# Experts' weights as 1 MB blocks of two neighbouring rows per partition, weight storage in 8 KB tiles

## The chip, the cores and the metric

The kernel runs on one core of one Trainium2 chip. The metric is the device time of one execution in microseconds (us). The engines are named as in the profile: PE multiplies matrices, PEld is its weight load, DVE, ACT and POOL are the vector, scalar and GpSimd engines, and SP issues the DMAs.

## What is computed

Two transformer blocks run one after the other on 512 tokens of width 1024, all in float32. The first block has two layers. Each layer has a mixer (latent attention beside a convolution), an attention over 256 memory rows, and a gated feed-forward part of width 2816. The second block is one layer: a gated delta-rule mixer with a pooling branch, and then a mixture of 16 experts. Each expert takes the 64 tokens with its highest affinity:

```python
aff = jax.nn.softmax((h @ w_router).astype(jnp.float32), axis=-1)
top_aff, top_idx = lax.top_k(jnp.swapaxes(aff, 1, 2), cap)          # cap = 2*512//16 = 64
xe = jax.vmap(lambda hb, ib: hb[ib])(h, top_idx)
hid = jax.nn.silu(einsum('becd,edf->becf', xe, w_gate)) * einsum('becd,edf->becf', xe, w_up)
ye = einsum('becf,efd->becd', hid, w_down) * top_aff[..., None]
# ... each expert's rows are added back to their tokens, scaled by a gate vector; then a final RMS norm
```

Each expert has three weight matrices of 1024 x 1024 in float32, so 48 matrices of 4 MB are read once.

## The kernel before, in words

The program is written as plain loops over tiles. A planner beneath it puts the instructions of each engine and of SP in an order, by its own costs and by when a tile's buffer is free; so an order in the trace need not be that of the source. A tile is asked for by a tag, and a tag has a fixed number of buffers. A buffer is free again when every instruction that touches its tile is done.

**Weights outside the experts.** `weight` (line 134) loads a piece of up to 128 x 1024 elements into a tile `wr` (5 buffers of 4 KB per partition), copies it rounded to a tile `wh` on ACT (line 148), and puts the rest into a tile `wl` on DVE or POOL (line 152). `wh` and `wl` have 4 buffers of 4 KB each. Three matmuls (`mm3`, lines 157 to 159) make one product. `kv_weight` (line 535) does the same for one matrix. `adaln` (line 902) loads its 48 pieces of `w_mod` into `wr` and multiplies them on DVE.

**The delta-rule part.** `delta_block` is run for eight blocks, four at a time (`lockstep`, line 1236). Each of the four has a scratch store for the whole of its run and passes it to the block that comes four later. The store is a `wr` buffer, taken by `block_store` (line 1229), and four are taken. Beside the blocks run the four `pool_branch` calls, one after the other. Each takes three tiles `s2` (11 buffers for all users), loads a small weight of 64 KB through `weight`, and multiplies. `delta_scan` follows.

**The experts** (`moe`, line 1614). `gather(q)` builds the inputs of four experts: the normalised tokens (two parts, `hh` and `hl`) are PE's stationary operand, and a 0/1 selection is the moving one (line 1732). ACT applies a scale and a shift per feature (line 1734). Feature k*128+p of the model lies on partition p of slice k. `hidden(e)` multiplies one expert's inputs by `w_gate` and `w_up`. The moving operand is a weight block in float32; the stationary one is 128 x 64, and each block is used by two matmuls that write the two halves of the partitions of one PSUM bank (lines 1762 and 1763):

```python
for ps, w in ((pg, A["w_gate_2"]), (pu, A["w_up_2"])):
    halves(ps, xe[:, k, e % 4, :], block(w, e, k), k == 0, k == 7)
```

Then come SiLU, a product, four transposes and a copy. `project(p)` multiplies two experts' results by `w_down` (line 1791). `combine(p)` adds the pair's rows to the tokens (line 1804 on PE, line 1812 on DVE), and `prepare(p)` makes the pair's combine matrix. In the loop `hidden(e)` comes first, then for even e `prepare` and the `project` of the pair before, for odd e its `combine`.

`block(w, e, k)` (line 1661) issues one DMA of 512 KB, 128 rows of 4 KB, one per partition. It goes to the next of 24 buffers of 4 KB per partition, taken in turn (`room`): 5 `wr`, 4 `wh`, 4 `wl`, one `nx`, and 10 halves of five larger tiles. There are 16 blocks for an expert's `hidden` and 8 for its part of `project`, 384 in all.

Of the kernel before, what the change touches and what calls it, by code (L numbers as in the profile page):

```python
# [10 lines left out]
F32 = mybir.dt.float32  # L11
F32R = mybir.dt.float32r
# [5 lines left out]
D = 1024  # L18
# [37 lines left out]

class Builder:
    N_N4 = 4
    N_WR = 5
    N_WH = 4  # L60

    def __init__(self, ctx, tc, A, out, dbg):
        self.tc, self.nc, self.A, self.out, self.dbg = tc, tc.nc, A, out, dbg
        self.cp = ctx.enter_context(tc.tile_pool(name="consts", bufs=1))
        self.sp = ctx.enter_context(tc.tile_pool(name="main", bufs=1))
        self.pp = ctx.enter_context(tc.tile_pool(name="psum", bufs=1, space=bass.MemoryType.PSUM))
        self.dp = ctx.enter_context(tc.tile_pool(name="dram", bufs=1, space=bass.MemoryType.DRAM))
        self.nw = 0
# [12 lines left out]
        self.xt = self.cp.tile([128, NT, D], F32, name="xt")  # L81
# [44 lines left out]
    def split_ps(self, ps, hi, lo, scale=None):  # L126
# [4 lines left out]
        else:  # L131
            nc.vector.scalar_tensor_tensor(lo, ps, scale, hi.bitcast(F32), op0=OP.mult, op1=OP.subtract)

    def weight(self, src, shape, raw=None, spare=False):

        nc = self.nc
        loaded = raw is not None
        if not loaded:
            raw = self.sp.tile([128] + list(shape), F32, name="wr", tag="wr", bufs=self.N_WR)
        if spare:  # L140
            hi, lo = self.n4(shape, F32R), self.n4(shape, F32R)
        else:
            hi = self.sp.tile([128] + list(shape), F32R, name="wh", tag="wh", bufs=self.N_WH)
        if not loaded:
            nc.sync.dma_start(raw, src)
        i = self.nw
        self.nw += 1
        nc.scalar.activation(hi, raw, AF.Copy)  # L148
        if not spare:
            lo = self.sp.tile([128] + list(shape), F32R, name="wl", tag="wl", bufs=self.N_WH)  # L150
# [287 lines left out]
    def mixer(self, l, xT):  # L438
# [94 lines left out]
        w_ukv = A["mla_w_ukv"][l].rearrange("(k p) (h d) -> p k h d", p=128, h=8)  # L533

        def kv_weight(d0):
            raw = self.sp.tile([128, 2, 512], F32, name="wr", tag="wr", bufs=self.N_WR)
            hi = self.sp.tile([128, 2, 512], F32R, name="wh", tag="wh", bufs=self.N_WH)
            lo = self.sp.tile([128, 2, 512], F32R, name="wl", tag="wl", bufs=self.N_WH)
# [363 lines left out]
    def adaln(self):  # L902
# [10 lines left out]
        for cc in range(12):  # L913
            cs = slice(cc * 512, (cc + 1) * 512)
            rs = (0, 1) if cc < 4 else (0,)
            acc = [self.s2([512]) for _ in rs]
            for k in range(0, 8, 2):
                wt = self.sp.tile([128, 2, 512], F32, name="wr", tag="wr", bufs=self.N_WR)
# [12 lines left out]
            nc.sync.dma_start(bm[0:1, :], A["b_mod_2"][0:1, cs])  # L931
            for r in rs:
                ps = self.pc()
                nc.tensor.matmul(ps[0:1, :], self.ones, acc[r], start=True, stop=True)
                o = self.s2([512])
                nc.vector.tensor_tensor(out=o[0:1, :], in0=ps[0:1, :], in1=bm[0:1, :], op=OP.add)
                nc.sync.dma_start(self.mod[r:r + 1, cs], o[0:1, :])
            yield

    def vectors2(self):  # L940
# [13 lines left out]
            nc.sync.dma_start(rows[8 + 16 * r:24 + 16 * r, :], k(self.mod[r, 0:2 * D]))  # L954
        nc.sync.dma_start(rows[40:48, :], k(A["norm2_2"][0]))
        nc.sync.dma_start(rows[48:64, :], k(self.mod[0, 3 * D:5 * D]))
        ps = self.pc()
        self.tr(ps[:, :64], rows[:64, :])
        v = self.c2.tile([128, 64], F32, name="mv")
        nc.vector.tensor_copy(v, ps[:, :64])  # L960

        wr = self.n4([8, 16])
        nc.sync.dma_start(wr, A["w_router_2"][0].rearrange("(k p) e -> p k e", p=128))
# [4 lines left out]
        self.rc = self.c2.tile([128, 16], F32, name="rc")  # L968
        nc.vector.tensor_copy(self.rc, ps[:, :16])

        a2 = self.c2.tile([128, 8], F32, name="a2")
        self.m2 = a2, v[:, 48:56]
# [256 lines left out]
    def block_store(self, w=None):  # L1229

        if w is None:
            w = self.sp.tile([128, 2, 4, 128], F32, name="wr", tag="wr", bufs=self.N_WR)
        self.nc.gpsimd.memset(w[:, 1], 0.0)
        return w

# [378 lines left out]
    def moe(self, cat):  # L1614
# [12 lines left out]
        def done(t, c):  # L1627
# [11 lines left out]
            if c == 0:  # L1639
# [11 lines left out]
        self.dump("x2", self.xt)  # L1651


        room = [self.sp.tile([128, D], F32, name=n, tag=n, bufs=k)
                for n, k in (("wr", self.N_WR), ("wh", self.N_WH), ("wl", self.N_WH), ("nx", 1)) for _ in range(k)]
        for _ in range(5):
            raw = self.t8([2, D], F32)
            room += [raw[:, 0], raw[:, 1]]
        turn = [0]

        def block(w, e, k):

            raw = room[turn[0] % len(room)]
            turn[0] += 1
            nc.sync.dma_start(raw, w[0, e, k * 128:(k + 1) * 128, :])
            return raw

        self.stage("wout")
# [48 lines left out]
        def gather(q):  # L1717
# [8 lines left out]
            for k in range(0, 8, 2):  # L1726
                ps = gring().rearrange("p (j n) -> p j n", j=2)
                for j in range(2):
                    ks = slice((k + j) * 128, (k + j + 1) * 128)
                    for i, src in enumerate((hh, hl)):  # L1730
                        for t in range(NT):
                            mm(ps[:, j, :], src[t // 2][:, t % 2, ks], oh[t // 2][:, t % 2],  # L1732
                               start=i + t == 0, stop=i + t == NT)
                    nc.scalar.activation(xe[:, k + j].rearrange("p e c -> p (e c)"), ps[:, j, :], AF.Identity,
                                         scale=a2[:, k + j:k + j + 1], bias=sh[:, k + j:k + j + 1])
                yield

        def prepare(p):
# [25 lines left out]

        def hidden(e, tokens=None):
            pg, pu = uring(), uring()
            for k in range(8):
                if tokens is not None and k % 2 == 0:
# [7 lines left out]
            ps = mring()  # L1776
            for j in range(4):
# [5 lines left out]
        def project(p):  # L1783

            hT = [hTs.pop(2 * p + j) for j in range(2)]
            pss = [dring(), dring()]
            for k in range(8):
                raw = [block(A["w_down_2"], 2 * p + j, k) for j in range(2)]
                for ps, cs in zip(pss, (c0, c1)):
                    for j, h in enumerate((lo_, hi_)):  # L1790
                        mm(ps[h, :], hT[j][:, k % 4, k // 4, :], raw[j][:, cs], start=k == 0, stop=k == 7)  # L1791
# [136 lines left out]
```

## Time and profile before

| | |
|---|---|
| time, three runs | 2574.59 us median (2574.55 to 2577.21) |
| profiled execution: its time / its span | 2574.39 us / 2572.2 us |
| mean granted PE clock | 0.975 |
| busy share of the span | PE 94%, PEld 70%, DVE 51%, ACT 35%, POOL 24% |
| DMA | 393.79 MB, mean 153 GB/s |

The profile is of one execution. "Busy" is the time an engine has an instruction in hand. The span is cut into 40 equal slices of 64.3 us, and a digit is the busy share of a slice in tenths. The experts' stage is the last eight of these slices. A wait is named by the instruction that waits and by what released it.

### The profile page before, as it was taken

How to read it: one execution, taken by the hardware profiler on the slowest of the kernel's cores; microseconds unless marked ns; L12 is line 12 of the kernel's file. 1: busy time of each engine (PE TensorE's matmuls, PEld its weight loads, DVE VectorE, ACT ScalarE, POOL GpSimd, SP SyncE). 2: the span in 40 equal slices, each digit the busy share in tenths (PEclk: the TensorE clock that was granted, in tenths of full speed). 3: DMA queues.
4: the chain of work that ended last, by engine and by line, in shares of the span. 5: the costliest groups of instructions: out<-in, count | busy, mean ns of one | idle time of the engine just before them, and what ended most of it. 6: DMA issues, size and time to landing. Idle time of an engine off the chain costs nothing.

```text
span 2572.2 us, 32232 instructions
## 1 busy us (share of the span) xinstructions
PE 2428.2 (94%) x12518; PEld 1795.3 (70%) x12518; DVE 1305.6 (51%) x2180; ACT 898.9 (35%) x1611; POOL 612.9 (24%) x467
## 2 busy tenths in 40 slices
PE   7989999999998979998999999989889789999997
PEld 6747888777777847887888888878788644343432
DVE  3977446754547785646554343466667511112112
ACT  4673442222222584433335343263562311010101
POOL 2872112221113583103122111223415000000000
PEclk9999999999999999999999999999889889999999
DMA  5312421554543311522232222221001489999996
GB/s 164 91 42 81 149 84 57 189 156 156 172 153 106 102 49 50 155 92 82 85 107 91 82 87 78 67 75 51 20 26 50 179 310 378 409 408 409 409 409 267
DMA packets 207060, 393.79 MB, mean 153 GB/s; under 512 B 24016, under 2 KB 115288, under 8 KB 206908
## 3 DMA queue, kind: packets, MB, share of 16 engines
q1 hardware_dynamic: 206908, 391.74, 43.7%
q8 instruction: 98, 1.61, 0.3%
q14 instruction: 54, 0.44, 0.0%
HBM read 389.56 MB, written 2.13 MB: 152 GB/s over the span
## 4 chain that ended last, share of the span: by engine, by line
PE 81%; DVE 12%; ACT 3%; DMA 2%; issue 1%; POOL 1%; SPq 0%; DVEq 0%; POOLq 0%; ACTq 0%
PE q L157 17%; PE q L159 17%; PE q L158 17%; PE q L1762 8%; PE q L1791 6%; PE q L163 3%; PE q L1732 2%; PE q L1804 1%; DVE wl L152 1%; PE q L1188 1%; PE q L1183 1%; DVE q L670 1%; PE q L1763 1%; DVE xt L281 1%; DVE s L1159 1%
## 5 line engine op out<-in xcount | busy, mean ns | idle before, releaser
L157 PE MATMUL q<-t,wh 128*128 128x512 f32 (+1 forms) x1320 | 491.7, 374 | 9.7 <-DVE t L130 4.4
L158 PE MATMUL q<-t,wh 128*128 128x512 f32 (+1 forms) x1320 | 491.0, 372 | 1.9 <-DVE t L1484 1.1
L159 PE MATMUL q<-t,wl 128*128 128x512 f32 (+1 forms) x1320 | 488.8, 372 | 0.5 <-DVE wl L152 0.5
L148 ACT ACTIVATE wh<-wr 128x1024 fp32r<-128x1024 f32 (+3 forms) x280 | 288.9, 1034 | 505.4 <-PE q L159 214.5
L157 PE MATMUL q<-wh,t 128*128 128x512 f32 (+4 forms) x964 | 365.5, 383 | 14.1 <-ACT wh L148 4.8
L152 DVE TENSOR_TENSOR wl<-wr,wh 128x1024 fp32r<-128x1024 f32 (+3 forms) x206 | 263.8, 1282 | 222.7 <-ACT wh L148 217.4
L158 PE MATMUL q<-wl,t 128*128 128x512 f32 (+4 forms) x964 | 362.1, 377 | 2.6 <-POOL wl L152 1.4
L159 PE MATMUL q<-wh,t 128*128 128x512 f32 (+4 forms) x964 | 358.6, 378 | 0.4 <-POOL t L1484 0.2
L152 POOL TENSOR_TENSOR wl<-wr,wh 128x1024 fp32r<-128x1024 f32 (+2 forms) x74 | 183.9, 2486 | 636.8 <-ACT wh L148 587.7
L157 PEld LDWEIGHTS q<-t,wh 128*128 128x128 f32 x1320 | 251.1, 191 | 58.3 <-DVE t L130 4.9
L158 PEld LDWEIGHTS q<-t,wh 128*128 128x128 f32 x1320 | 251.3, 190 | 44.5 <-DVE t L1484 1.4
L159 PEld LDWEIGHTS q<-t,wl 128*128 128x128 f32 x1320 | 251.2, 190 | 42.0 <-DVE wl L152 1.4
L185 POOL TENSOR_TENSOR sm<-sm,mhalf 128x1 f32<-128x1 f32 (+3 forms) x75 | 71.8, 959 | 768.8 <-DVE sm L183 764.8
L157 PEld LDWEIGHTS q<-wh,t 128*128 128x128 f32 x964 | 183.5, 191 | 57.3 <-DVE xt L292 6.0
L158 PEld LDWEIGHTS q<-wl,t 128*128 128x128 f32 x964 | 183.7, 191 | 34.8 <-POOL wl L152 1.9
L159 PEld LDWEIGHTS q<-wh,t 128*128 128x128 f32 x964 | 182.7, 190 | 35.5 <-issue 0.9
L680 POOL TENSOR_TENSOR t<-t,cm 128x511 f32<-128x511 f32 (+14 forms) x120 | 147.9, 1233 | 22.3 <-ACT cm L677 16.8
L801 POOL TENSOR_TENSOR t<-cm,t 128x512 fp32r<-128x512 f32 x44 | 70.4, 1600 | 303.3 <-ACT t L800 303.3
L163 PE MATMUL q<-ident,s 128*128 128x128 f32 (+3 forms) x506 | 90.6, 287 | 50.4 <-DVE s L1694 13.1
L163 PEld LDWEIGHTS q<-ident,s 128*128 128x128 f32 (+3 forms) x506 | 60.6, 143 | 104.6 <-ACT s L609 26.5
L1763 PE MATMUL q<-t,t 128*64 128x512 f32 x272 | 127.6, 600 | 0.0
L1762 PE MATMUL q<-t,t 128*64 128x512 f32 x272 | 127.2, 598 | 0.0
(445 smaller groups left out, 3665.0 us busy)
## 6 DMA issues: line engine op xcount, KB each, us to landing
wr<-in_ffn_w_in SPq DMA_DIRECT2D x88, 512.0 KB
t<-in_w_gate SPq DMA_DIRECT2D x68, 512.0 KB
t<-in_w_up SPq DMA_DIRECT2D x68, 512.0 KB
wr<-in_w_mod SPq DMA_DIRECT2D x48, 512.0 KB
wr<-in_ffn_w_down SPq DMA_DIRECT2D x44, 512.0 KB
wr<-in_w_down SPq DMA_DIRECT2D x35, 512.0 KB
wr<-in_xa_w_kv SPq DMA_DIRECT2D x32, 512.0 KB
wl<-in_w_down SPq DMA_DIRECT2D x32, 512.0 KB
```

Of the source, the lines that this page charges most:

```text
L148: nc.scalar.activation(hi, raw, AF.Copy)
L152: e.tensor_tensor(out=lo, in0=raw, in1=hi.bitcast(F32), op=OP.subtract)
L157: m(out, ah, bh, start=first, stop=False)
L158: m(out, ah, bl, start=False, stop=False)
L159: m(out, al, bh, start=False, stop=last)
L163: self.nc.tensor.transpose(out, in_, self.ident[:n, :n])
L185: nc.gpsimd.tensor_tensor(out=r, in0=v, in1=self.mhalf[:, :n], op=OP.pow)
L680: nc.gpsimd.tensor_tensor(out=acc[:, i, d:], in0=acc[:, i, d:], in1=m, op=OP.add)
L801: nc.gpsimd.tensor_tensor(out=hl[:, j + i, :], in0=sg, in1=hh[:, j + i, :].bitcast(F32), op=OP.subtract)
L1762: mm(ps[lo_, :], x, raw[:, c0], start=first, stop=last)
L1763: mm(ps[hi_, :], x, raw[:, c1], start=first, stop=last)
L1791: mm(ps[h, :], hT[j][:, k % 4, k // 4, :], raw[j][:, cs], start=k == 0, stop=k == 7)
```

## The change

**Blocks.** `block(w, e, j)` loads 256 rows of a matrix as 1 MB: partition p takes the two neighbouring rows 256j+2p and 256j+2p+1, which lie one behind the other in memory. There are 192 blocks. `room` has 12 buffers of 8 KB: 3 `wr`, 4 `wh` and five larger tiles; `nx` and `wl` are gone. Each block is used for its first rows and then for its second (r = 0, 1).

**Order of the features.** So that operands fit, `gather` takes every second feature as stationary operand (a step of two elements), the transposes in `hidden` read every second column, and the scale and shift vectors are needed in that order as well: `vectors2` loads them a second time with six small DMAs, and its transposed tile has 88 columns instead of 64.

**Storage.** `wr` has 3 buffers of 8 KB, and `raw4` hands out their halves in turn, across all users. `wh` has 4 buffers of 8 KB that hold both parts, the rounded one and the rest.

```diff
-    N_WR = 5
+    N_WR = 3
+    def raw4(self, shape):
+        if self.nraw % 2 == 0:
+            self.rawt = self.sp.tile([128, 2, D], F32, name="wr", tag="wr", bufs=self.N_WR)
+        half = self.rawt[:, self.nraw % 2, :int(np.prod(shape))]
+        self.nraw += 1
+        return half if len(shape) == 1 else half.rearrange("p (a b) -> p a b", a=shape[0])
+    def parts(self, shape):
+        t = self.sp.tile([128, 2, D], F32R, name="wh", tag="wh", bufs=self.N_WH)
+        out = [t[:, i, :int(np.prod(shape))] for i in range(2)]
+        ...
     def weight(self, src, shape, raw=None, spare=False):
...
-            raw = self.sp.tile([128] + list(shape), F32, name="wr", tag="wr", bufs=self.N_WR)
+            raw = self.raw4(shape)
...
-            hi = self.sp.tile([128] + list(shape), F32R, name="wh", tag="wh", bufs=self.N_WH)
+            hi, lo = self.parts(shape)
...
     def block_store(self, w=None):
-            w = self.sp.tile([128, 2, 4, 128], F32, name="wr", tag="wr", bufs=self.N_WR)
+            w = self.raw4([1024]).rearrange("p (a b c) -> p a b c", a=2, b=4)
...
     # vectors2
+        for i, ap in enumerate((A["norm2_2"][0], self.mod[0, 3 * D:4 * D], self.mod[0, 4 * D:5 * D])):
+            for r in range(2):
+                nc.sync.dma_start(rows[64 + 8 * i + 4 * r:68 + 8 * i + 4 * r, :],
+                                  ap.rearrange("(j p r) -> r j p", p=128, r=2)[r])
...
     # moe
-        def block(w, e, k):
+        def block(w, e, j):
...
-            nc.sync.dma_start(raw, w[0, e, k * 128:(k + 1) * 128, :])
+            nc.sync.dma_start(raw, w[0, e, j * 256:(j + 1) * 256, :].rearrange("(p r) d -> p r d", r=2))
...
     # gather
+                            x = src[t // 2][:, t % 2].rearrange("p (j q r) -> p j r q", q=128, r=2)
+                            mm(ps[:, r, :], x[:, j, r, :], oh[t // 2][:, t % 2], start=i + t == 0, stop=i + t == NT)
...
     # hidden
-                    halves(ps, xe[:, k, e % 4, :], block(w, e, k), k == 0, k == 7)
+                    raw = block(w, e, j)
+                    for r in range(2):
+                        halves(ps, xe[:, 4 * r + j, e % 4, :], raw[:, r], j + r == 0, j + r == 4)
...
-                self.tr(ps[:, j * 128:(j + 1) * 128], u[:, j * 128:(j + 1) * 128])
+                self.tr(ps[:, j * 128:(j + 1) * 128], uv[:, j // 2, j % 2, :])
...
     # project
-            for k in range(8):
-                raw = [block(A["w_down_2"], 2 * p + j, k) for j in range(2)]
+            for i in range(4):
+                raw = [block(A["w_down_2"], 2 * p + j, i) for j in range(2)]
+                for r in range(2):
+                    for ps, cs in zip(pss, (c0, c1)):
+                        for j, h in enumerate((lo_, hi_)):
+                            mm(ps[h, :], hT[j][:, i % 2 * 2 + r, i // 2, :], raw[j][:, r, cs],
+                               start=i + r == 0, stop=i + r == 4)
```

The places in `kv_weight` and `adaln` that took a `wr` tile call `raw4` in the same way, and the first calls `parts`.

## Rows read from the trace of the kernel before

**Rows 1.** The page: span, busy time per engine, DMA share in 40 slices
```profile
span 2572.2 us, 32232 instructions
...
PE 2428.2 (94%) x12518; PEld 1795.3 (70%) x12518; DVE 1305.6 (51%) x2180; ACT 898.9 (35%) x1611; POOL 612.9 (24%) x467
...
DMA  5312421554543311522232222221001489999996
```

**Rows 2.** The page: chain that ended last, by engine
```profile
PE 81%; DVE 12%; ACT 3%; DMA 2%; issue 1%; POOL 1%; SPq 0%; DVEq 0%; POOLq 0%; ACTq 0%
```

**Rows 3.** Windows: from:to, length, busy PE PEld DVE ACT POOL (count), clock, DMA share, GB/s
```profile
480.00:540.00 60.00, 60.00 (x250) 45.46 (x249) 40.68 (x55) 14.30 (x17) 16.25 (x6) 1.00 0.53 167
...
1860.00:1940.00 80.00, 73.08 (x658) 68.66 (x657) 52.01 (x117) 49.42 (x126) 12.19 (x10) 0.87 0.07 21
...
2065.00:2553.00 488.00, 486.26 (x2076) 191.92 (x2076) 82.25 (x150) 51.91 (x87) 0.00 (x0) 0.99 0.98 389
...
2220.00:2260.00 40.00, 39.99 (x166) 14.61 (x165) 7.86 (x16) 3.55 (x6) 0.00 (x0) 1.00 1.03 409
```

**Rows 4.** Waits of PEld, 2200 to 2545: who for what, us, times, longest
```profile
PEld q L1762 <- issue: 61.5, 209, 0.8
...
PEld q L1762 <- DMA wr<-in_w_down: 3.7, 13, 0.3
...
PEld q L1791 <- DMA t<-in_w_down: 1.8, 3, 0.8
```

**Rows 5.** Waits of SP's own queue, 2000 to 2560
```profile
SPq L1665 <- PE q L1763: 81.9, 101, 19.2
SPq L1665 <- DMA t<-in_w_up: 45.7, 52, 0.9
```

**Rows 6.** Timeline: buffer nx loaded, read, loaded anew (start, duration, idle before)
```profile
2276.28 0.33 SPq L1665 DMA_DIRECT2D nx<-in_w_up  x1
...
2305.34 0.14 PEld L1762 LDWEIGHTS q<-nx,t 128*64 128x64 f32 x1 [0.29 <-DMA wh<-in_w_down]
2305.77 0.14 PEld L1762 LDWEIGHTS q<-nx,t 128*64 128x64 f32 x1 [0.29 <-issue]
...
2306.84 0.33 SPq L1665 DMA_DIRECT2D nx<-in_w_down  x1
```

**Rows 7.** Timeline of SP: two loads issued one after the other
```profile
2322.02 0.33 SPq L1665 DMA_DIRECT2D wr<-in_w_up  x1
2323.30 0.33 SPq L1665 DMA_DIRECT2D wr<-in_w_gate  x1
```

**Rows 8.** The chain in order of time, at the end: start, us, what
```profile
2539.33 13.88 PE q L1791 x60
```

**Rows 9.** Groups by line and form, 2100 to 2540: busy us, mean ns
```profile
L1732 PEld LDWEIGHTS q<-s,t 128*128 128x128 f32 x192 | 24.5, 189 | 20.3 <-issue 19.5 <-ACT t L1734 0.8
```

**Rows 10.** Line 1142: stationary operand is one column repeated; ns min/median/max
```profile
L1142 PEld LDWEIGHTS q<-trif,gla x48: 185/190/192, 1376.8 to 1884.5; 128*128 128x128 f32 x48
```

**Rows 11.** Two lines of vectors2: SP's issues
```profile
L956 SPq DMA_DIRECT2D s<-mod x1: 309/309/309, 1153.7 to 1153.7; - x1
...
L963 SPq DMA_DIRECT2D n<-in_w_router x1: 368/368/368, 1233.8 to 1233.8; - x1
```

**Rows 12.** The page: the split of weights on ACT, count and idle time
```profile
L148 ACT ACTIVATE wh<-wr 128x1024 fp32r<-128x1024 f32 (+3 forms) x280 | 288.9, 1034 | 505.4 <-PE q L159 214.5
```

**Rows 13.** Waits of SP's own queue, 1780 to 1990
```profile
SPq L1372 <- POOL s L1419: 26.3, 2, 21.2
```

**Rows 14.** Lines of pool_branch on DVE: ns min/median/max, first to last start
```profile
L1413 DVE TENSOR_TENSOR s<-n,s x2: 675/684/693, 1830.2 to 1907.0; 128x512 f32<-128x512 f32 x2
...
L1414 DVE TENSOR_TENSOR s<-s,t x2: 691/796/900, 1838.8 to 1907.7; 128x512 f32<-128x512 f32 x2
...
L1419 DVE TENSOR_TENSOR s<-s,s x2: 681/687/693, 1845.2 to 1935.0; 128x512 fp32r<-128x512 f32 x2
```

**Rows 15.** Timeline of PEld where combine cuts in
```profile
2215.67 0.19 PEld L1804 LDWEIGHTS q<-n,s 128*128 128x128 f32 x1 [0.81 <-ACT n L1796]
```

More of the change, by code (lines that the diff above doesn't have):

```diff
@@ L67, in __init__ @@
         self.dp = ctx.enter_context(tc.tile_pool(name="dram", bufs=1, space=bass.MemoryType.DRAM))
-        self.nw = 0
+        self.nw = self.nraw = 0
         self.wp, self.np, self.c2 = None, 0, self.cp
@@ L132, in split_ps @@
             nc.vector.scalar_tensor_tensor(lo, ps, scale, hi.bitcast(F32), op0=OP.mult, op1=OP.subtract)
+    def raw4(self, shape):
[7 more added lines that the diff above has]
+        out = [t[:, i, :int(np.prod(shape))] for i in range(2)]
+        return out if len(shape) == 1 else [x.rearrange("p (a b) -> p a b", a=shape[0]) for x in out]
     def weight(self, src, shape, raw=None, spare=False):
@@ L148, in weight @@
         nc.scalar.activation(hi, raw, AF.Copy)
-        if not spare:
-            lo = self.sp.tile([128] + list(shape), F32R, name="wl", tag="wl", bufs=self.N_WH)
         e = nc.gpsimd if self.pool_lo and i % self.pool_lo == self.pool_lo - 1 else nc.vector
@@ L535, in kv_weight @@
         def kv_weight(d0):
-            raw = self.sp.tile([128, 2, 512], F32, name="wr", tag="wr", bufs=self.N_WR)
-            hi = self.sp.tile([128, 2, 512], F32R, name="wh", tag="wh", bufs=self.N_WH)
-            lo = self.sp.tile([128, 2, 512], F32R, name="wl", tag="wl", bufs=self.N_WH)
+            raw = self.raw4([2, 512])
+            hi, lo = self.parts([2, 512])
             for k in range(2):
@@ L917, in adaln @@
             for k in range(0, 8, 2):
-                wt = self.sp.tile([128, 2, 512], F32, name="wr", tag="wr", bufs=self.N_WR)
+                wt = self.raw4([2, 512])
                 nc.sync.dma_start(wt, w[k * 128:(k + 2) * 128, cs].rearrange("(k p) f -> p k f", p=128))
@@ L956, in vectors2 @@
         nc.sync.dma_start(rows[48:64, :], k(self.mod[0, 3 * D:5 * D]))
+        for i, ap in enumerate((A["norm2_2"][0], self.mod[0, 3 * D:4 * D], self.mod[0, 4 * D:5 * D])):
+            for r in range(2):
+                nc.sync.dma_start(rows[64 + 8 * i + 4 * r:68 + 8 * i + 4 * r, :],
+                                  ap.rearrange("(j p r) -> r j p", p=128, r=2)[r])
         ps = self.pc()
-        self.tr(ps[:, :64], rows[:64, :])
-        v = self.c2.tile([128, 64], F32, name="mv")
-        nc.vector.tensor_copy(v, ps[:, :64])
+        self.tr(ps[:, :88], rows[:88, :])
+        v = self.c2.tile([128, 88], F32, name="mv")
+        nc.vector.tensor_copy(v, ps[:, :88])
         wr = self.n4([8, 16])
@@ L969, in vectors2 @@
         nc.vector.tensor_copy(self.rc, ps[:, :16])
-        a2 = self.c2.tile([128, 8], F32, name="a2")
-        self.m2 = a2, v[:, 48:56]
+        a2p = self.c2.tile([128, 8], F32, name="a2")
+        self.m2 = a2p, v[:, 72:80]
+        nc.vector.scalar_tensor_tensor(a2p, v[:, 80:88], 1.0, v[:, 64:72], op0=OP.add, op1=OP.mult)
+        a2 = self.sm([8])
         nc.vector.scalar_tensor_tensor(a2, v[:, 56:64], 1.0, v[:, 40:48], op0=OP.add, op1=OP.mult)
@@ L1651, in moe @@
         self.dump("x2", self.xt)
[L1654 to L1658, printed above, removed]
+        room = [self.sp.tile([128, 2, D], F32, name=n, tag=n, bufs=k)
+                for n, k in (("wr", self.N_WR), ("wh", self.N_WH)) for _ in range(k)]
+        room += [self.t8([2, D], F32) for _ in range(5)]
         turn = [0]
-        def block(w, e, k):
+        def block(w, e, j):
             raw = room[turn[0] % len(room)]
             turn[0] += 1
-            nc.sync.dma_start(raw, w[0, e, k * 128:(k + 1) * 128, :])
+            nc.sync.dma_start(raw, w[0, e, j * 256:(j + 1) * 256, :].rearrange("(p r) d -> p r d", r=2))
             return raw
@@ L1725, in gather @@
             a2, sh = self.m2
[L1726 to L1729, printed above, removed]
+            for j in range(4):
+                ps = gring().rearrange("p (r n) -> p r n", r=2)
+                for r in range(2):
                     for i, src in enumerate((hh, hl)):
                         for t in range(NT):
[L1732 to L1735, printed above, removed]
+                            x = src[t // 2][:, t % 2].rearrange("p (j q r) -> p j r q", q=128, r=2)
+                            mm(ps[:, r, :], x[:, j, r, :], oh[t // 2][:, t % 2], start=i + t == 0, stop=i + t == NT)
+                    k = 4 * r + j
+                    nc.scalar.activation(xe[:, k].rearrange("p e c -> p (e c)"), ps[:, r, :], AF.Identity,
+                                         scale=a2[:, k:k + 1], bias=sh[:, k:k + 1])
                 yield
@@ L1766, in hidden @@
             pg, pu = uring(), uring()
-            for k in range(8):
-                if tokens is not None and k % 2 == 0:
+            for j in range(4):
+                if tokens is not None:
                     next(tokens)
@@ L1776, in hidden @@
             ps = mring()
+            uv = u.rearrange("p (b q r) -> p b r q", q=128, r=2)
             for j in range(4):
-                self.tr(ps[:, j * 128:(j + 1) * 128], u[:, j * 128:(j + 1) * 128])
+                self.tr(ps[:, j * 128:(j + 1) * 128], uv[:, j // 2, j % 2, :])
             hT = self.s2([4, 2, CAP])
@@ L1786, in project @@
             pss = [dring(), dring()]
-            for k in range(8):
-                raw = [block(A["w_down_2"], 2 * p + j, k) for j in range(2)]
-                for ps, cs in zip(pss, (c0, c1)):
-                    for j, h in enumerate((lo_, hi_)):
-                        mm(ps[h, :], hT[j][:, k % 4, k // 4, :], raw[j][:, cs], start=k == 0, stop=k == 7)
+            for i in range(4):
+                raw = [block(A["w_down_2"], 2 * p + j, i) for j in range(2)]
+                for r in range(2):
+                    for ps, cs in zip(pss, (c0, c1)):
+                        for j, h in enumerate((lo_, hi_)):
+                            mm(ps[h, :], hT[j][:, i % 2 * 2 + r, i // 2, :], raw[j][:, r, cs],
+                               start=i + r == 0, stop=i + r == 4)
             y = [self.n4([D], F32R) for _ in range(2)]
```

## The prediction

> **What bounds the kernel now.** I read four views in this order. The page first: the reader is to see that PE is busy for 2428 of 2572 us, and that the DMA line reads 9 only in the last slices, where the experts run [rows 1]. The chain that ended last lies 81% on PE and 2% on a DMA [rows 2]. So PE is the first suspect everywhere, and the experts' stage has two: PE and the loads.
>
> The windows show both at their limit in that stage. From 2065 to 2553 PE is busy for 486.3 of 488 us, and from 2220 to 2260 the DMA engines are at a share of 1.03 with 409 GB/s [rows 3]. A share cannot tell which of them sets the pace; the waits can. From 2200 to 2545 PE's weight loads wait for a DMA in pieces of 0.3 us, which is also the idle time ahead of a load that waits for nothing, and one piece of 0.8 us stands out [rows 4]. SP's queue waits for PE 101 times, 81.9 us in all: it wants to load and finds no free buffer [rows 5]. The clearest sight is one buffer. `nx` is loaded at 2276.28, read at 2305.34 and loaded anew at 2306.84, as soon as PE lets go [rows 6]. That is 29 us from issue to use, while loads go out every 1.28 us [rows 7], which is 512 KB at 409 GB/s. About 23 loads are ahead of PE. The chain ends in the same way: 60 matmul records of the last `project` in one piece of 13.88 us, 0.23 us each, without a wait [rows 8].
>
> So PE sets the pace and the loads keep up with little to spare. A block costs PE 0.86 us: its two matmuls run side by side, each is recorded twice, and pairs follow at 0.43 us (2305.34 to 2305.77) [rows 6]. The 384 blocks are 329 us of the stage's 488; gathering, combining, transposes and changes between them fill the rest.
>
> **The change, part by part.** The sum is made against the profiled execution, 2574.4 us with a span of 2572.2; the median of the runs is 2574.6, so the two can be taken as one.
>
> *1 MB blocks.* 192 loads replace 384, with the same bytes. SP saves 192 issues of 0.33 us [rows 7], which nothing waits for. A row of 8 KB instead of two of 4 KB should move a little faster. In a stretch whose rows are 1 and 2 KB the engines spend 0.53 x 16 x 4096 / 167 = 208 ns for 4 KB; with 4 KB rows they spend 1.03 x 16 x 4096 / 409 = 165 ns [rows 3]. The difference is spread over at most three further row starts, so one start costs about 14 ns, and 8 KB costs 316 to 330 ns in place of 330: the loads get 0 to 4.3% faster (an estimate from these two rows). As PE sets the pace, what comes back is what PE waits for loads: at most the 1.7 us that it is not busy [rows 3], and I take -1.3.
>
> The Trainium skill ("DMA: Bandwidth & Descriptors", section "Rules for kernel authors") asks for at least 1 MiB per DMA, and its table of measured sizes gives 341 GB/s for 1 MB alone. The trace does not agree that the size of one DMA is the limit here: 512 KB loads with several in flight move 409 GB/s. By that rule the change would pay through the loads, which is rival B.
>
> *Room for blocks.* 24 x 4 KB become 12 x 8 KB. A buffer comes free only after twice as many matmuls, which takes 0 to 2 small blocks from a lead of about 23; the lead covers it, and 2.6 us (two loads) is the price if it did not.
>
> *The end.* After the last landing eight matmul groups are left instead of four, +1.7 us at 0.43 us a record pair, if PE were waiting for that load. It is not: 15 blocks' work (60 records) is queued there [rows 8]. I take 0.
>
> *Stationary operands with a step of two.* 256 loads in `gather` and 64 in the transposes. The trace has no such load. The nearest rows are a contiguous load, 189 ns [rows 9], and one whose operand is one column repeated, 190 ns [rows 10]: the way of reading the operand didn't show. The lower end is 0. The upper end is every load twice as long, 320 x 0.189 us = +60 us, as PE has no idle time to hide it. I take 0, nearest to the row with another step.
>
> The Trainium skill ("SBUF — State Buffer", section "Door 1: The DMA port swizzle") says that two float32 in one 16-byte line are enough for full bandwidth. A step of two gives just that, so by the page the sum is the same 0; no run here shows it yet.
>
> *Vectors a second time.* Six more small DMAs stand behind the one at 1153.7, and what uses the tile comes at about 1234 [rows 11]. Six issues at 0.31 us are 1.9 us; even four times that is covered by the 80 us between. 0.
>
> *wh and wl in one tile.* Both parts were freed by the same three matmuls. 0.
>
> *wr as halves of three tiles.* Six halves in place of five, but a pair comes free together and pairs mix users. Outside the delta-rule part, four split weights lie between the load and PE, so I take 0, with 3 us to either side for stage starts. In the delta-rule part the count matters. ACT splits 280 weights into `wh` [rows 12], and 5 more go to spare tiles; less 8 for `w_out` and 4 for the pools, 273 came before. With 4 of `kv_weight` and 48 of `adaln` that makes 325 halves, an odd number. So the four block stores start in the second half of a tile: they touch three tiles, and those are all there are. The first pool weight fits into the last half. The second to fourth must wait until the second four delta blocks are done, near 1942. Before, one of five buffers stayed free and the pool weights passed through it.
>
> What is late next: the pool branches. The last already prepares its input as late as 1935 [rows 14]. Moved behind 1942, its three DVE steps of 0.68, 0.80 and 0.69 us come into the scan, where DVE is on the chain: 0 to +2.2, and I take +2.2. PE then needs the pool results only for `w_out`, near 1990. The dearer end is rival C.
>
> Sum: 2574.4 - 1.3 + 2.2 = 2575.3, I say 2575.5.
>
> **Rivals.**
>
> B, *the loads set the pace after all* (2558). Speaks for it: 409 GB/s without a dip for most of the stage. Against: the 29 us between load and use, and SP's waits for PE. If the 367 us from 2180 to 2547 ran at the pace of the loads, 4.3% would come back: -16 us.
>
> B2, *the planner packs the work better* (2565). A change of kind of matmul costs PE about 0.5 us: 0.81 us idle against 0.29 [rows 6, 15]. With larger blocks it may cut in less often. Twenty times less is -10 us. Nothing in the profile says that it will.
>
> C, *the pool branches hold tiles that the delta blocks need* (2593). Each branch that waits for its weight keeps two `s2` tiles of 11, and each of four live blocks needs two. These tiles are short already: SP waits 26.3 us for one that a branch holds [rows 13]. If a second branch takes two before the second four blocks have theirs, two blocks have to wait for the others' end. The window from 1860 to 1940 has PE busy for 73 of 80 us [rows 3]; half of it run again without overlap would be 40 us, and nothing if the blocks come first. I take +18. It decides from three branches' worth of tiles held at about 1896. Against it: blocks come earlier in the source.
>
> D, *stepped operands load slowly* (2634): the +60 us above, in `gather`, from any slowdown on, since PE is never idle there.
>
> E, *the rows of 8 KB don't come about* and the DMA engines still move 4 KB at a time. Then the term of -1.3 goes and the time is 2577: it lies inside the forecast and has no chance of its own.
>
> **How the numbers follow.** A measurement of this kernel can tell about 0.2% (5.1 us) from no change. Forecast 0.50 (own range 2569 to 2583: the 3 us of stage starts, 2.6 of room, and a reordered queue), B 0.15, B2 0.06, C 0.23, D 0.06. Faster: 0.06 of the forecast, 0.14 of B, 0.05 of B2 = 0.25. Same: 0.36, 0.01, 0.01 and 0.02 of C = 0.40. Slower: 0.08, 0.21 of C, 0.06 of D = 0.35. The range takes in B and most of C and leaves out D: 2556 to 2597.
>
> **What would show it.** Right: the experts' stage again about 488 us with PE busy throughout, loads at up to 425 GB/s but with gaps, SP waiting for PE more than now; line 1732's weight loads at 189 ns; pool weights two to four issued after the second four delta blocks; the stretch from 1860 to 1990 within 3 us of before. Wrong: an experts' stage shorter by over 6 us (B or B2, told apart by PE's idle time and the number of changes), weight loads over 250 ns in `gather` (D), or a longer delta-rule part (C).

## The result, and the profile after

The changed kernel takes 2588.1 us median (2585.8 to 2589.7), the kernel before beside it 2574.6: a ratio of 1.0051, interval 1.0040 to 1.0063. It is slower by 13.5 us. The profiled execution took 2588.3 us.

The page of the changed kernel: span, busy time, DMA share in 40 slices, chain that ended last by engine. It answers to [rows 1, 2].

```profile
span 2586.5 us, 31702 instructions
...
PE 2434.2 (94%) x12518; PEld 1809.4 (70%) x12518; DVE 1307.0 (51%) x2181; ACT 898.2 (35%) x1611; POOL 613.4 (24%) x467
...
DMA  4302422544543311422332222221011479999995
...
PE 81%; DVE 10%; ACT 4%; DMA 2%; issue 2%; POOL 2%; SPq 0%; DVEq 0%; POOLq 0%; ACTq 0%
```

The page shows little: the same busy shares, 14 us more span. The windows show where (columns as in [rows 3]; the experts' window is moved with the stage):

```profile
480.00:540.00 60.00, 60.00 (x251) 45.48 (x251) 44.75 (x60) 14.77 (x18) 17.80 (x6) 1.00 0.54 183
1860.00:1940.00 80.00, 73.20 (x652) 68.61 (x651) 50.21 (x118) 48.76 (x127) 14.87 (x12) 0.91 0.09 28
1940.00:1990.00 50.00, 42.03 (x279) 38.25 (x280) 26.47 (x42) 10.94 (x21) 13.05 (x12) 0.80 0.16 56
2084.00:2567.00 483.00, 474.55 (x2076) 193.96 (x2076) 80.72 (x150) 51.80 (x87) 0.00 (x0) 0.99 0.95 393
2220.00:2260.00 40.00, 38.49 (x168) 14.25 (x166) 8.64 (x13) 3.05 (x5) 0.00 (x0) 1.00 1.01 426
```

The kernel before, the third of these windows:

```profile
1940.00:1990.00 50.00, 48.05 (x376) 44.64 (x375) 41.06 (x61) 8.95 (x17) 29.86 (x23) 1.00 0.20 64
```

From 1860 to 1940 PE is as busy as before. From 1940 to 1990 PE does 279 instructions in place of 376, at a granted clock of 0.80 in place of 1.00. That is the delta-rule part; PE is busy for 42.0 of these 50 us in place of 48.1. `pos`, the end of the routing, comes at 2083.9 in place of 2065.1: 18.8 us later. The experts give back 4.6: the same 2076 matmul records take 483 us in place of 488 [rows 3], and from `pos` to the first output it is 491.8 in place of 496.4. The two rows of each timeline (start, duration, engine and line, what; in brackets the idle time before and what ended it), the kernel before:

```profile
2065.07 0.23 DVE L1710 TENSOR_TENSOR pos<-q,mk 128x64 f32<-128x64 f32 x1 [2.11 <-PE q L1708]
...
2561.47 7.44 SPq L1852 DMA_DIRECT2D out<-t  x4
```

The changed one:

```profile
2083.93 0.23 DVE L1726 TENSOR_TENSOR pos<-q,mk 128x64 f32<-128x64 f32 x1 [2.10 <-PE q L1724]
...
2575.70 7.44 SPq L1873 DMA_DIRECT2D out<-t  x4
```

The cause of the 18.8 us lies in a few more rows of its timeline. First SP's loads in this stretch:

```profile
1792.49 0.34 SPq L159 DMA_DIRECT2D wr<-in_pool_w  x1
...
1928.97 5.33 SPq L159 DMA_DIRECT2D wr<-in_pool_w  x3
1934.35 37.17 SPq L159 DMA_DIRECT2D wr<-in_w_out  x8
```

Then PE:

```profile
1932.02 0.48 PE L169 MATMUL q<-s,wh 128*128 128x512 f32 x1
...
1936.76 1.10 PE L1206 MATMUL q<-wr,s 128*128 128x64 f32 x8 [2.10 <-ACT t L1441]
...
1966.95 1.11 PE L1243 MATMUL q<-wr,s 64*64 64x64 f32 x8
```

The second pool weight is loaded at 1928.97, when the first of the second four delta blocks has let go of its store. Its product follows at 1932.02, its copy out of PSUM (ACT, line 1441) ends at 1936.7. Only then does the fourth of these blocks run its first level (line 1206); it was ready for it from 1904 on. Its last step starts at 1966.95; the other three blocks were done by 1933.6. The source says why: the pool branches and every fourth delta block take their PSUM banks, in which PE's products lie until they are copied out, in turn from one ring of two, `rg[3]`. The branch has the next bank and waits for its weight; the block behind it waits for the branch.

The experts' stage of the changed kernel: waits of PEld from 2200 to 2545 (who for what, us, times, longest).

```profile
PEld q L1778 <- issue: 83.1, 286, 0.4
```

Waits of PE itself, 2084 to 2576:

```profile
PE q L175 <- DVE s L1793: 5.2, 6, 0.9
PE q L1825 <- ACT n L1817: 2.6, 4, 0.6
```

The kernel before, 2065 to 2562:

```profile
PE q L1804 <- ACT n L1796: 0.9, 4, 0.2
```

The changed kernel again, waits of SP's own queue, 2000 to 2560:

```profile
SPq L1681 <- PE q L1779: 267.5, 124, 30.7
SPq L1681 <- PE q L1811: 126.9, 51, 9.3
```

Its chain in order of time, near the end:

```profile
2553.56 13.88 PE q L1811 x60
```

PEld's waits for a DMA are gone [rows 4], and so are SP's: they summed to 259 us in the kernel before, of which [rows 5] shows one line, and sum to 1 us now. SP waits for these matmuls 394 us in place of 98 (81.9 in [rows 5] and 16.4 for line 1791): the loads move 426 GB/s and stand still more often. PE itself waits longer for DVE and ACT, where a transpose or `combine` comes before its operand. PE is idle for 8.5 us of this stage in place of 1.7. The end is the same 13.88 us [rows 8].

### The profile page after: what moved, and what is told of

It reads as the page before. It is cut to its first block, busy times and chain, and to the rows that moved or that the text cites. A ratio compares the mean times of both kernels' runs of the same rounds, so it can differ in the third digit from the quotient of the medians.

```text
span 2586.5 us, 31702 instructions
## 1 busy us (share of the span) xinstructions
PE 2434.2 (94%) x12518; PEld 1809.4 (70%) x12518; DVE 1307.0 (51%) x2181; ACT 898.2 (35%) x1611; POOL 613.4 (24%) x467
## 4 chain that ended last, share of the span: by engine, by line
PE 81%; DVE 10%; ACT 4%; DMA 2%; issue 2%; POOL 2%; SPq 0%; DVEq 0%; POOLq 0%; ACTq 0%
PE q L169 17%; PE q L171 17%; PE q L170 17%; PE q L1778 8%; PE q L1811 5%; PE q L175 4%; DVE wh L164 1%; PE q L1748 1%; PE q L1201 1%; PE q L1825 1%; PE q L1206 1%; DVE q L681 1%; POOL t L691 1%; PE q L1779 1%; DVE xt L293 1%
## 5 line engine op out<-in xcount | busy, mean ns | idle before, releaser
L169 PE MATMUL q<-t,wh 128*128 128x512 f32 (+1 forms) x1320 | 490.8, 373 | 13.3 <-DVE t L130 4.4
L170 PE MATMUL q<-t,wh 128*128 128x512 f32 (+1 forms) x1320 | 490.6, 372 | 1.9 <-DVE t L1502 1.1
L171 PE MATMUL q<-t,wh 128*128 128x512 f32 (+1 forms) x1320 | 487.7, 372 | 0.1
L169 PE MATMUL q<-wh,t 128*128 128x512 f32 (+4 forms) x964 | 366.8, 384 | 17.6 <-ACT wh L162 8.6
L164 DVE TENSOR_TENSOR wh<-wr,wh 128x1024 fp32r<-128x1024 f32 (+3 forms) x206 | 267.6, 1300 | 217.0 <-ACT wh L162 210.7
L170 PE MATMUL q<-wh,t 128*128 128x512 f32 (+4 forms) x964 | 364.0, 379 | 1.5 <-DVE wh L164 1.3
L171 PE MATMUL q<-wh,t 128*128 128x512 f32 (+4 forms) x964 | 359.7, 379 | 0.2 <-POOL t L1502 0.2
L164 POOL TENSOR_TENSOR wh<-wr,wh 128x1024 fp32r<-128x1024 f32 (+2 forms) x74 | 183.4, 2480 | 648.7 <-ACT wh L162 545.9
L169 PEld LDWEIGHTS q<-t,wh 128*128 128x128 f32 x1320 | 251.1, 191 | 62.9 <-DVE t L130 4.9
L170 PEld LDWEIGHTS q<-t,wh 128*128 128x128 f32 x1320 | 251.3, 190 | 43.5 <-DVE t L1502 1.4
L171 PEld LDWEIGHTS q<-t,wh 128*128 128x128 f32 x1320 | 251.0, 190 | 42.2 <-DVE wh L164 1.0
L169 PEld LDWEIGHTS q<-wh,t 128*128 128x128 f32 x964 | 184.2, 191 | 59.5 <-ACT wh L162 10.7
L170 PEld LDWEIGHTS q<-wh,t 128*128 128x128 f32 x964 | 184.6, 192 | 35.8 <-DVE wh L164 2.6
L171 PEld LDWEIGHTS q<-wh,t 128*128 128x128 f32 x964 | 184.1, 191 | 35.0 <-issue 0.9
L1779 PE MATMUL q<-t,t 128*64 128x512 f32 x272 | 124.1, 596 | 0.0
L1778 PE MATMUL q<-t,t 128*64 128x512 f32 x272 | 123.8, 596 | 0.0
```

The source lines that it names most:

```text
L169: m(out, ah, bh, start=first, stop=False)
L170: m(out, ah, bl, start=False, stop=False)
L171: m(out, al, bh, start=False, stop=last)
L1778: mm(ps[lo_, :], x, raw[:, c0], start=first, stop=last)
L1779: mm(ps[hi_, :], x, raw[:, c1], start=first, stop=last)
```

## Experiments

**What holds the fourth block?** Theory 1: the PSUM bank, behind a weight that waits for a `wr` tile. Theory 2: `s2` tiles held by the branches, as rival C had it.

*One half skipped* (ahead of the stores):

```diff
+        self.nraw += self.nraw % 2
         store = [self.block_store() for _ in range(4)]
```

> The changed kernel with one half of a `wr` tile skipped ahead of the four block stores, so that they fill two tiles and the third holds the first two pool weights. Theory 1 (the second pool weight waits for a `wr` tile, and its product holds a PSUM bank that the fourth delta block needs next): the second weight is loaded near 1800 us in place of 1928.97, the last delta block ends near 1942 in place of 1967.8, `pos` is written near 2065 in place of 2083.9, and the time falls by about 19 us to 2569 (2566 to 2573). If the odd count of halves is not the reason (the planner's order, or anything else in the change): the time stays at 2588 (2585 to 2590) although the second weight is early.

Measured: 2578.8, ratio 1.0013 (1.0004 to 1.0022).

*Pools first*:

```diff
+        self.pw = self.raw4([4, 128])
+        nc.sync.dma_start(self.pw, A["pool_w_2"][0].rearrange("g p f -> p g f"))
         store = [self.block_store() for _ in range(4)]
...
-        wh, wl = self.weight(A["pool_w_2"][0, g], [128])
+        wh, wl = self.weight(None, [128], raw=self.pw[:, g])
```

> The changed kernel with all four pool weights loaded by one DMA into one half of a `wr` tile ahead of the four block stores; no pool weight waits for a tile. Theory 1: as with the skipped half, 2569 us (2566 to 2573); as the third and fourth weight are early too, up to 2 us less than there. If only w_out's late loads cost the time (they wait for the stores' tiles here as well): 2588.

Measured: 2579.1, ratio 1.0016 (1.0007 to 1.0025). In both the stall is gone: the pool weights are loaded by 1808, the last block ends at 1947, `pos` comes at 2066.6 and 2065.6. Two rows of the first of them:

```profile
1796.38 11.81 SPq L159 DMA_DIRECT2D wr<-in_pool_w  x4
...
1946.85 0.68 PE L1243 MATMUL q<-wr,s 64*64 64x64 f32 x8
```

So the odd count is the reason for 17 to 18 of the 18.8 us. But the time fell by 9 us and not by 19: from `pos` to the first output both need 497.9 us, 6 more than the changed kernel. What the experts gave back there was gone as well.

*Pool branch in `cm`* (its line for mh and ml takes tiles of tag `cm`):

> The changed kernel, its odd count kept, with the two parts of a pool branch's input (mh, ml) in the two `cm` tiles, which nothing else uses there, in place of two `s2` tiles. Theory 1 (PSUM bank): the fourth delta block's first level still starts near 1937 us, the time stays at 2588 (2585 to 2591). Theory 2 (the waiting branches hold `s2` tiles that the delta blocks need, as rival C had it): the stall goes, 2570 (2567 to 2574).

Measured: 2589.6, ratio 1.0054 (1.0040 to 1.0067). PE's row of the fourth block's first level in this run:

```profile
1936.68 1.00 PE L1206 MATMUL q<-wr,s 128*128 128x64 f32 x8
```

The same as before the edit: theory 2 falls.

*Late bank*:

```diff
         wh, wl = self.weight(A["pool_w_2"][0, g], [128])
+        for _ in range(4 if g == 1 else 0):
+            yield
         ps = ring()
```

> The changed kernel, its odd count and its `s2` tiles kept; the second pool branch asks for its PSUM bank four turns later than its weight and its `s2` tiles, so that the fourth delta block's bank comes before it. Its weight still waits for a tile until near 1930 us. Theory 1 (PSUM bank): the fourth block's first level starts near 1905 us in place of 1936.8, and the time falls to 2569 to 2574 (the third and fourth branch come some 8 turns later, which may cost the 2 us for their DVE steps). Theory 2 (`s2` tiles): the stall stays, 2588 (2585 to 2591).

Measured: 2570.9, ratio 0.9986 (0.9977 to 0.9995). The weights come as late as ever, and the last of the blocks no longer cares (timeline of this run, SP's pool loads and the blocks' last step on PE):

```profile
1934.51 4.86 SPq L159 DMA_DIRECT2D wr<-in_pool_w  x3
...
1941.81 0.68 PE L1243 MATMUL q<-wr,s 64*64 64x64 f32 x8
```

Theory 1 holds.

**What is the change worth without the stall?**

*The kernel before with the late bank* (the same two lines):

> The kernel before with the late bank alone: the second pool branch asks for its PSUM bank four turns later, as in the late-bank run; nothing of the change. Theory: the late bank saves the 2.5 us by which `pos` came earlier there (2062.6 for 2065.1) in this kernel too, so 2572 (2570 to 2574), and what the late-bank run has over it is the change's own worth in the experts' stage, 1 to 2 us. Rival: the kernel before gains nothing (2574.5), and the 4 us that the late-bank run is faster all come from the change.

Measured: 2565.1, ratio 0.9957 (0.9945 to 0.9970). Both expectations put its worth too low: the late bank gives the kernel before 10 us. Why it helps there, where no pool weight is late, was not traced. Its profiled execution took 2561.9, the shortest of its runs; in it `pos` comes at 2058.1, 7 us earlier, and the experts take 5.5 us less. Against it the change with a late bank is slower by 5.9 us, and the intervals don't touch.

*Storage alone* (blocks, gathering, vectors as before; the late bank in):

```diff
+        room = [t[:, i] for t in room for i in range(2)]
...
-            nc.sync.dma_start(raw, w[0, e, j * 256:(j + 1) * 256, :].rearrange("(p r) d -> p r d", r=2))
+            nc.sync.dma_start(raw, w[0, e, k * 128:(k + 1) * 128, :])
```

> The late-bank kernel with the change's storage alone: `wr` and `wh` in tiles of 8 KB as changed, but blocks of 512 KB, contiguous operands, the order of features and the vectors as before. The late-bank run took 2570.9 us and the kernel before with a late bank 2565.1, with `pos` at 2062.8 and 2058.3. If storage (w_out's loads wait for whole tiles) makes those 6 us: 2569 to 2571 here too, `pos` near 2062. If the blocks make them: 2565 (2563 to 2567).

Measured: 2571.5, ratio 0.9987 (0.9978 to 0.9995), `pos` at 2063.3. The storage, or the order that the planner makes with it, makes the loss. The blocks, rows and features together are worth 0.6 us, which cannot be told from nothing. In the profiled executions, 8.2 us apart, 5.2 us of the loss lie ahead of `pos` and 3.3 behind (494.2 from there to the first output, for 490.9). Where the first part arises is seen only so far: the last sum of the scan's outputs starts at 1990.8 in place of 1985.3, and three pool weights are loaded at 1935 to 1941 in place of by 1812. That the one makes the other was not tried.

**What sets the pace of the experts?**

*Two DMAs for a block*:

```diff
-            nc.sync.dma_start(raw, w[0, e, j * 256:(j + 1) * 256, :].rearrange("(p r) d -> p r d", r=2))
+            for r in range(2):
+                nc.sync.dma_start(raw[:, r], w[0, e, j * 256:(j + 1) * 256, :].rearrange("(p r) d -> r p d", r=2)[r])
```

> The late-bank kernel with each block of 1 MB loaded by two DMAs of 512 KB, each with rows of 4 KB (one of the two neighbouring rows per partition); tiles, operands and matmuls stay. If PE sets the pace of the experts' stage: the loads fall from 426 to some 409 GB/s, the packets are of 4096 bytes, the stage after `pos` stays at 495 us (493 to 498) and the time at 2571 (2569 to 2574). If the loads set it: the stage gets longer by up to 4% of the 420 us in which they run, to 2580 to 2588.

Measured: 2572.6, ratio 0.9990 (0.9981 to 0.9999): as the late-bank run. The loads' speed is not on the path. It was 418 GB/s, not 409.

*Fewer loads*:

```diff
-                for ps, w in ((pg, A["w_gate_2"]), (pu, A["w_up_2"])):
-                    raw = block(w, e, j)
+                raw = block(A["w_gate_2"], e, j)
+                for ps in (pg, pu):
```

> The late-bank kernel with w_up left out of the loads: the matmuls of w_up use the block of w_gate, so 128 blocks are loaded in place of 192 and the matmuls are as many. If PE sets the pace: PE has all its work as before and the time stays at 2571 (2567 to 2574, the planner's order being another). If the loads set it: the stage shrinks to what PE needs, which would show as PE idle now, 20 us or more: 2550 or less.

Measured: 2540.8, ratio 0.9868 (0.9854 to 0.9881). By my expectation that would be the loads' pace. The windows contradict it. The whole stage in the late-bank run:

```profile
2063.00:2557.00 494.00, 481.54 (x2096) 197.09 (x2096) 84.10 (x156) 56.74 (x101) 0.55 (x1) 1.00 0.92 384
```

And in this one:

```profile
2067.00:2529.00 462.00, 458.87 (x2096) 187.49 (x2096) 84.96 (x158) 57.31 (x104) 0.62 (x2) 0.99 0.70 265
```

PE runs the same 2096 records and is busy for 22.7 us less, though it never waited long for a DMA in either. So PE's work is no fixed sum, and both branches of my expectation had taken it for one. The other 9.3 us of the shorter stage are PE's idle time, 3.1 us in place of 12.5. Of the 22.7 us, 19.6 are on one line. Windows again, now of w_down's line only (busy PE and PEld, clock, DMA share, GB/s). The kernel before gives 164.6 us; the changed one:

```profile
2084.00:2571.00 487.00, 151.58 (x512) 48.21 (x512) 0.99 0.94 389
```

The late-bank run:

```profile
2063.00:2557.00 494.00, 153.40 (x512) 48.57 (x512) 1.00 0.92 384
```

The run with fewer loads:

```profile
2067.00:2529.00 462.00, 133.79 (x512) 38.74 (x512) 0.99 0.70 265
```

512 records need between 134 and 165 us. The timeline of the late-bank run says how:

```profile
2109.52 0.59 PE L1780 MATMUL q<-wh,t 128*64 128x512 f32 x1
2109.53 0.59 PE L1781 MATMUL q<-wh,t 128*64 128x512 f32 x1
2109.95 0.59 PE L1780 MATMUL q<-wh,t 128*64 128x512 f32 x1
...
2122.80 3.65 PE L1813 MATMUL q<-wr,s 128*64 128x512 f32 x12
```

Two matmuls that write the two halves of the partitions start 0.01 us apart and share a slot of 0.43 us. The twelve records of w_down take 3.65 us, which are eight slots: four shared, four with one record alone. The two halves belong to two experts, whose blocks come by two loads, and in PE's order one expert's matmuls often stand without the other's. Counted over the stage (alone: no other such record starts within 0.2 us), 153 of w_down's 512 records ran alone in the kernel before, 138 in the changed one, 166 with pools first, 154 with the late bank, 38 with fewer loads; slots of 0.43 us in all, 854, 844, 852, 848 and 804, where 768 would do. (The Trainium skill, "TensorE: Matmul & The Clock Gate", section "Part 3: Packing small matmuls — row/col tiling", has it that matmuls on different column groups of the array run at the same time. The trace agrees, 0.01 us apart, for neighbours in PE's order.)

*Contiguous operands*:

```diff
-                            x = src[t // 2][:, t % 2].rearrange("p (j q r) -> p j r q", q=128, r=2)
+                            x = src[t // 2][:, t % 2].rearrange("p (j r q) -> p j r q", q=128, r=2)
...
-            uv = u.rearrange("p (b q r) -> p b r q", q=128, r=2)
+            uv = u.rearrange("p (b r q) -> p b r q", q=128, r=2)
```

> The late-bank kernel with contiguous stationary operands in place of those with a step of two, in the 256 loads of the gathering and the 64 transposes (so the features reach the wrong weight rows); nothing else moves. If the step costs what the means of the trace say (206 for 201 ns in the gathering, 185 for 140 ns in the transposes): 256 x 0.005 + 64 x 0.045 = 4 us less in the stage at most, 2567 to 2570, and the transposes' loads are back at 140 ns. If the step costs nothing and the means differ by what the loads stand beside: 2571 (2570 to 2572).

Measured: 2570.7 against 2570.9. PE's order is the same in both, so their weight loads compare one to one. Groups by line and form, 2100 to 2540 (busy us, mean ns), in the late-bank run:

```profile
L1750 PEld LDWEIGHTS q<-s,t 128*128 128x128 f32 x192 | 24.3, 196 | 12.2 <-issue 12.2
...
L175 PEld LDWEIGHTS q<-ident,s 128*128 128x128 f32 x92 | 11.7, 184 | 25.2 <-DVE s L1795 12.2 <-issue 8.1 <-DVE s L1761 4.1
```

In the contiguous one:

```profile
L1750 PEld LDWEIGHTS q<-s,t 128*128 128x128 f32 x192 | 24.0, 190 | 12.2 <-issue 12.2
...
L175 PEld LDWEIGHTS q<-ident,s 128*128 128x128 f32 x96 | 10.0, 140 | 26.0 <-DVE s L1795 12.2 <-issue 8.9 <-DVE s L1761 4.1
```

The step is real: 6 ns a load in gathering, and more in a transpose's load than the means say. The group of 92 mixes 60 stepped loads of `hidden`, 194 to 222 ns, mean 208, with 32 contiguous ones of `prepare`, mean 141; without the step all take 140. Its cost in time is below what can be measured.

**Pairs that come together.**

*Paired w_down*:

```diff
+            nc.sync.dma_start(raw, A["w_down_2"][0, 2 * p:2 * p + 2, k * 128:(k + 1) * 128, :].rearrange("e p d -> p e d"))
...
-                raw = [block(A["w_down_2"], 2 * p + j, i) for j in range(2)]
+                raw = pair_block(p, k)
```

> The late-bank kernel with w_down loaded for both experts of a pair by one DMA of 1 MB (128 rows of 4 KB from each), so that the matmuls of the two experts, which write the two halves of the partitions and can run side by side, become ready together; the transposes in `hidden` are contiguous again, w_gate and w_up stay at 8 KB rows. In the late-bank run 154 of 512 such matmuls ran alone, in the experts' stage 848 slots of 0.43 us where 768 would do. Theory: it is the order that sets PE's time there; fewer than 20 run alone, some 75 slots less, -32 us by PE alone, but then the loads get scarce (180 blocks after the first twelve, 120 of 2.46 us and 60 of 2.56 us, 449 us from 2072 on, and some 28 us after them): 2548 (2538 to 2556). Rival: matmuls that run alone cost nothing because the loads set the pace anyway: 2568 to 2573.

Measured: 2556.2, ratio 0.9927 (0.9913 to 0.9940): faster than both kernels, and than the kernel before with the late bank. Eight records ran alone, 772 slots. W_down's line in windows:

```profile
2067.00:2545.00 478.00, 121.86 (x512) 34.37 (x512) 0.99 0.95 397
```

The whole stage:

```profile
2067.00:2545.00 478.00, 451.81 (x2097) 178.56 (x2096) 84.97 (x159) 57.33 (x103) 0.55 (x1) 0.99 0.95 397
```

Two of the waits from 2060 to 2560, SP's queue first:

```profile
SPq L1683 <- DMA wh<-in_w_down: 33.9, 23, 2.2
```

Then PEld:

```profile
PEld q L1787 <- DMA t<-in_w_up: 8.9, 7, 1.4
```

W_down takes 31.5 us less. But PE is idle for 26.2 us in place of 12.5, and PEld's waits for a DMA sum to 27 us: now the loads hold PE up, and some 14 us of the gain go there. So the stage from `pos` on is 17 us shorter. SP's own waits for a DMA, 162 us, are no sign of the pace: the kernel before had 259 us of them with PE busy throughout, and the run with rows of 4 KB below has 9. Of the 8 us above the forecast, 4.5 are a later `pos` (below); the other 4 were not traced.

*The same with pools first*:

> As the run with paired w_down, and all four pool weights loaded by one DMA ahead of the block stores, as in the pools-first run; `pos` comes at 2060 to 2063. Theory: within 3 us of the run with paired w_down. It is to be the fastest of these kernels if the early w_out loads, which the late bank alone does not bring, are worth what the storage costs.

Measured: 2558.5, ratio 0.9938 (0.9926 to 0.9951): within 3 us, not the fastest. `pos` came at 2069.1 and not at 2060 to 2063, so what early loads of `w_out` are worth is not shown.

*Rows of 4 KB*:

```diff
-            nc.sync.dma_start(raw, w[0, e, j * 256:(j + 1) * 256, :].rearrange("(p r) d -> p r d", r=2))
+            nc.sync.dma_start(raw, w[0, e, j * 256:(j + 1) * 256, :].rearrange("(r p) d -> p r d", r=2))
```

> The run with paired w_down, and a block of w_gate or w_up takes the rows p and p+128 of its 256 in place of two neighbouring ones: still one DMA of 1 MB, but in rows of 4 KB; gathering (contiguous again), scale and shift follow that order, and PE has the same instructions in the same order. In the paired run the loads are scarce: SP waits for DMAs over 150 us in all and PE over 25 us. Theory: the rows alone give 409 GB/s in place of 426, the 120 loads take 2.56 us in place of 2.46, +12 us, all of it on the path: 2568 (2562 to 2571). If rows of 8 KB don't make the 426 GB/s, or PE still sets the pace: 2556 (2554 to 2558).

Measured: 2560.4, ratio 0.9943 (0.9929 to 0.9957): between the two expectations and in neither's range. From `pos` to the first output the profiled execution is 5.0 us longer (482.7 for 477.7); the times differ by 4.2 us, and their intervals overlap. So rows of 8 KB seem to pay here, some 5 us and not 12, by one profile each. A window of the paired run:

```profile
2310.00:2370.00 60.00, 55.50 (x262) 21.27 (x260) 11.64 (x22) 6.51 (x11) 0.00 (x0) 1.00 1.02 425
```

And of this one:

```profile
2310.00:2370.00 60.00, 52.76 (x246) 19.64 (x244) 11.64 (x22) 5.98 (x11) 0.00 (x0) 1.00 1.02 419
```

4 KB rows move 419 GB/s in these tiles, not the 409 that I had taken from [rows 3].

## What the prediction had wrong, and where it was right

- **The number.** 2588.1 us lies in the stated range, 2556 to 2597, but 5 us above the forecast's own, 2569 to 2583. The range reaches so far only for rival C, and C's cause did not occur: that it holds is partly luck.
- **The step that failed** is "*wr as halves of three tiles*" with its "what is late next". The count of 325, the straddling stores and the late second to fourth weight were right (1928.97 for my "near 1942"). But I let only the branch's own DVE steps fall behind the late weight, 0 to +2.2 us, and that was the mis-read: behind it stood a PSUM bank and behind the bank a whole delta block. The stall cost 17 to 18 us of the 18.8 up to `pos` (half skipped, pools first). What would have shown it is in the source, `rg[3]` for both; no row that I had read could, since in the kernel before the weight was never late.
- **Rival C** had the right place, near the right size (+18) and the right first cause, and the wrong thing held: `s2` tiles are not it (pool branch in `cm`), the bank is (late bank). Its own sign, a longer delta-rule part, is what came.
- **The experts' stage** came 4.6 us shorter, where I had 1.3. Not as loads: two DMAs per block cost nothing measurable. Ten slots fewer are 4.3 us, and PE changes 176 times between these matmuls and others in place of 220; 6.7 us more of waiting go against it. Rival B2 foresaw the fewer changes, but its price of 0.5 us for each is not borne out: with the stall removed in two ways PE changes 174 times, and the stage, at 852 slots, was 1.5 us longer than before. So the 4.6 us are luck of the order; storage alone against all of the change differs by 0.6 us.
- **PE sets the pace**: right for the changed kernel. [Rows 5] were read one-sidedly for it: beside SP's 81.9 us for PE the same view has 259 us for DMAs. I read PE's 486 busy us as work, too, and some 35 us of them (82 slots more than the paired run's) were records that ran alone; [rows 8] shows the good case, 60 records at 0.23 us each, and I took it for the rule (384 x 0.86 is 330 us; 854 slots of 0.43 are 367). **Rival B** was wrong here and comes true once PE is relieved.
- **8 KB rows**: 426 for 409 GB/s is +4.2%, the upper end of my 0 to 4.3%. About half of it is not the rows: 4 KB rows moved 417 to 419 in the new tiles.
- **The step of two, rival D**: 0 was right as time. The rule cited from the Trainium skill ("SBUF — State Buffer", section "Door 1: The DMA port swizzle"), full rate for two float32 in a line, is not what the runs show: 190 to 196 ns in gathering, and 140 to 208 ns in the transposes.
- **Size of a DMA**: 512 KB and 1 MB loads with 4 KB rows move the same 418 and 419 GB/s here (two DMAs; rows of 4 KB). The rule of 1 MiB from the Trainium skill ("DMA: Bandwidth & Descriptors", section "Rules for kernel authors") shows no effect here, with several loads in flight.
- **Room, end, vectors**: 0 fits, though none was tried by itself. Up to 1770 us the changed kernel is mostly 1 to 1.5 us behind, with some 4 us between 800 and 950 that it wins back.

## What to carry to other kernels

When a buffer gets scarcer, list not only who will wait for it but what the waiter already holds, PSUM banks too; whoever is next in that ring waits as well. A busy PE is not a fixed amount of work: matmuls on half of the array cost double when their partner is not next to them, and loading both partners by one DMA put them there. A small change moves the planner's order everywhere, so one kernel's 5 us in a stage it hardly touched should be tested with the order held.

## What I had not expected of the hardware

- The same 512 KB loads with 4 KB rows move 409 GB/s in the kernel before, with the late bank too, and 417 in the storage-alone run, where they go to halves of 8 KB tiles. What makes the difference stays open. Storage alone:

```profile
2220.00:2260.00 40.00, 39.99 (x171) 15.17 (x171) 6.37 (x14) 4.11 (x7) 0.00 (x0) 1.00 1.03 417
```

- The granted clock can drop in one execution and not in another with the same order on PE. The late-bank run, within the multiplication by `w_out`:

```profile
2010.00:2020.00 10.00, 10.00 (x53) 8.33 (x53) 4.06 (x5) 2.90 (x8) 0.84 (x1) 1.00 0.48 197
```

The one with contiguous operands:

```profile
2010.00:2020.00 10.00, 10.00 (x37) 8.09 (x37) 2.47 (x4) 1.72 (x6) 0.34 (x1) 0.67 0.45 184
```

The 0.67 is a mean over its two levels, 1.2 and 2.4 GHz. In the first PE had been idle for 1.5 of the 10 us before, in the second for 1.0. From the first transpose near 2007 to the last product with the router's weights the two took 35.5 and 38.6 us. The paired run had the low clock there too. It puts some 3 us on `pos` that belong to no edit.
